# A hybrid decoder step on one core: prompt attention's sums of values in undivided float32, two tiles of keys in the two halves of TensorE's columns

## The chip, the cores and the metric

The program runs on 1 core of one Trainium2 chip. The time is device microseconds of one execution; lower is better. All times below are of this one core.

## The reference, cut to what matters

One decoder layer runs on 1024 prompt tokens and on 8 sampled tokens with 8192 tokens of cache each. The prompt's attention has three branches (compressed keys, selected blocks, a window of 512), 8 heads in 2 groups and a head size of 64. For 1024 tokens all 16 blocks are selected, so the selected branch is plain causal attention over all keys. Each branch takes a softmax, and the three sums of values are gated and added:

```python
s_c = jnp.einsum('bqgrd,bcgd->bgrqc', q, kc).astype(f32) + bias_c
p_c = jax.nn.softmax(jnp.where(valid_c, s_c, NEG), axis=-1) * valid_c
o_c = jnp.einsum('bgrqc,bcgd->bqgrd', p_c.astype(vc.dtype), vc)
...
o_s = jnp.einsum('bgrqk,bgqkd->bqgrd', p_s.astype(v_sel.dtype), v_sel)
...
o_w = jnp.einsum('bgrql,blgd->bqgrd', p_w.astype(vw.dtype), vw)
g = jax.nn.sigmoid(gates)
o = g[..., 0:1] * o_c + g[..., 1:2] * o_s + g[..., 2:3] * o_w
```

Everything is float32.

## The kernel before

The kernel goes through projections, retention, keys and values, then a stage in which the prompt's attention is woven together with the compression of the 8 caches and the sampled tokens' attention, and then output projection, feed-forward network and embedding. Large products are made in a split form: a float32 operand x is kept as hi = x rounded to float32r and lo = x - hi, and products of such parts are added up in PSUM. Other products (the compression, L944, the transposes, L1144) take undivided float32 operands.

**Prompt attention** works in 32 units: 8 tiles i of 128 queries, 2 groups, 2 pairs of heads. A unit has two heads, so the moving operand of its sums of values is 128 keys by 256 (two heads by 128 queries). `near_scores` and `far_scores` make scores, exponentials (ScalarE) and the scaling by gate and sum; `near_values` sums the compressed tile and up to 5 tiles of the window, `far_values` sums i + 1 tiles of keys. Both call `values`, which takes the tiles of keys two at a time (a part): PE transposes the probabilities of a part into a PSUM tile `t` (L1144); ScalarE casts them to `ph` (L1149), VectorE subtracts to get `pl` (`sub` at L142); `products` then multiplies. Over a unit the parts number half its tiles, rounded up, for near and far each: 80 near and 80 far parts in all, 136 of two tiles and 24 of one, 296 tiles.

In `products` the stationary operand is a tile of values from `vst` or `cvst`: 128 keys by 128 columns, the 64 hi columns and the 64 lo columns side by side. It is multiplied once with `ph` and once with `pl`; the PSUM bank `o` thus has the hi part of the values in its rows 0 to 63 and the lo part in its rows 64 to 127, and `far_values` adds the two halves (`ot`, `mo`).

**The stage's other work on PE.** The compression's products (L944, 128 by 128 stationary, 256 moving columns, float32), transposes and score products of the sampled tokens (L1258, L1268), and the compression's tails (L1200, and L1207 with L1208). L1200, L1207 with L1208, and L1268 already write two halves: each pair has two stationary operands of 64 columns, one for PSUM rows 0 to 63 and one for rows 64 to 127 of the same bank.

**What sets the order.** `weave` calls the generators of the stage by the costs that they yield; a list scheduler in the framework then sets each engine's final order. Each engine runs its own list strictly in that order and waits on semaphores. PSUM tiles `t` have 2 buffers, `o` has 1, `ph` and `pl` have 2 each.

Of the kernel before, what the change touches and what calls it, by code (L numbers as in the profile page):

```python
# [11 lines left out]
F32R = mybir.dt.float32r  # L12
# [28 lines left out]
def f32(ap):  # L41
    return ap.bitcast(F32)
# [78 lines left out]
def hybrid_kernel(tc, I, C, O):  # L121
    nc = tc.nc
    V, G, A, P, SY = nc.vector, nc.gpsimd, nc.scalar, nc.tensor, nc.sync
# [6 lines left out]
    def tl(pool, shape, tag, dt=F32, bufs=None):  # L130
        kw = {} if bufs is None else {"bufs": bufs}
        return pool.tile(shape, dt, tag=tag, name=nm(tag), **kw)
# [8 lines left out]
    def sub(eng, out, a, b):  # L141
        eng.tensor_tensor(out=out, in0=a, in1=b, op=ALU.subtract)  # L142
# [537 lines left out]
    for pair in range(2):  # L680
        rqk = tl(pr, [128, 2, 2, T], "rqk", bufs=1)
        rgs = tl(pr, [128, 2, T], "rgs", bufs=1)
        if pair:
# [3 lines left out]
            for t in range(9):  # L687
                pt, r = tok_major(wts, 256, t)
# [12 lines left out]
    pq = pool("pq", side="right")  # L701
# [1 line left out]
    pcv = pool("pcv", side="right")  # L703
    pat = pool("pat", side="right")
    ckst = [tl(pat, [128, 64], f"ckst{g}", F32R) for g in range(2)]
    cvst = tl(pat, [128, 2, 128], "cvst", F32R)
    cfar = const(pat, "cfar")
    rowv = const(pat, "rowv")
    vst = tl(pq, [128, 2, 8, 2, 128], "vst", F32R)

    kst = [tl(pq, [128, 2, S], f"kst{g}", F32R) for g in range(2)]
    pb = pool("pb")
# [41 lines left out]
    def keys_values(kind, ncol):  # L754
        wts = w_take()
        pend, kds = [], []

        def turn(t, pair):
            cs = slice((t - 1) * 128, (t + 1) * 128)
            ptr = bank("t", 2)  # L760
            for i in range(2):
                P.transpose(ptr[:, i * 128:(i + 1) * 128], pair[i], ident)
            for g in range(2):
                gh, gl = slice(g * 64, g * 64 + 64), slice(64 - g * 64, 128 - g * 64)
                A.copy(kst[g][gh, kind, cs], ptr[gh, :256])
                sub(V, kst[g][gl, kind, cs], ptr[gh, :256], f32(kst[g][gh, kind, cs]))

        for t in (8, *range(8)):
            pt, r = tok_major(wts, ncol, t)
            kv = tl(pb, [128, 256], "kv", bufs=4)  # L770
            A.copy(kv[:r], pt[:r, 0:256])
            if kind == 1:
                th = tl(pb, [128, 24], "gth", bufs=2)
                A.activation(th[:r], pt[:r, 256:280], AF.Tanh, scale=0.5)
            vr = kv[:, 128:256]
            if t < 8:
                hi, lo = vst[:, kind, t, :, 0:64], vst[:, kind, t, :, 64:128]
                vr3 = vr.rearrange("p (g d) -> p g d", g=2)
                A.copy(hi, vr3)
                sub(V, lo, vr3, f32(hi))  # L780
            else:
                A.copy(vnew[:, kind, :], vr[:r])
            sq = tl(pb, [128, 128], "sq", bufs=1)
            A.activation(sq[:r], kv[:r, 0:128], AF.Square)
            ssk = tl(pb, [128, 2], "ssk", bufs=2)
            V.reduce_sum(ssk[:r], sq[:r].rearrange("p (g d) -> p g d", g=2), axis=AX)
            rsqrt_small(ssk[:r], ssk[:r], 1.0 / 64, 2, r)
            t1 = tl(pb, [128, 2, 64], "kt1", bufs=2)
            mul(V, t1[:r], kv[:r, 0:128].rearrange("p (g d) -> p g d", g=2), ssk[:r].unsqueeze(2).to_broadcast([r, 2, 64]))
            ko = tl(pb, [128, 2, 64], "ko", bufs=4)  # L790
            mul(V, ko[:r], t1[:r], kn_bc[:r].unsqueeze(1).to_broadcast([r, 2, 64]))
            kflat = ko[:r].rearrange("p g d -> p (g d)")
            names = ("slc_k", "slc_v") if kind == 0 else ("win_k", "win_v")
            for n, src in zip(names, (kflat, vr[:r])):
                if t == 8:
                    dst = O["s_" + n][0, :, 0] if kind == 0 else O["s_" + n][0, :, 511]
                elif kind == 0:
                    dst = O["p_" + n][0, 0, t * 128:(t + 1) * 128]
                elif t >= 4:
                    dst = O["p_" + n][0, 0, t * 128 - 512:(t + 1) * 128 - 512]  # L800
                else:
                    continue
                SY.dma_start(dst.rearrange("t g d -> t (g d)"), src)
            if kind == 1:
                G.tensor_scalar(gsig[:r, t, :], th[:r], 0.5, 0.5, op0=ALU.mult, op1=ALU.add)
            if 3 <= t < 7:
                w_split()
            yield 2700.0
            if t == 8:
                knew = kflat  # L810
            if t == 0:
                ptr = bank("t", 2)
                P.transpose(ptr[:, :8], knew, ident[:8, :8])
                V.tensor_copy(knT[:, kind, :], ptr[:, :8])
            if pend and t % 2 == 0:
                turn(*pend)
                pend = []
            if t < 8:
                kds.append(kflat)
                if t % 2 == 1:  # L820
                    pend, kds = (t, kds), []
        yield 1500.0
        turn(*pend)
# [33 lines left out]
    def prompt_blocks():  # L857
        staged = stage_w1(pb, pcw, 0)
        for kv in (0, 1):
# [28 lines left out]
            if kv == 0:  # L888
                sq = tl(ptb, [64, 2, 64], "csq")
                A.activation(sq, pt3, AF.Square)  # L890
                ssk = tl(ptb, [64, 2], "css")
                V.reduce_sum(ssk, sq, axis=AX)
                rsqrt_small(ssk, ssk, 1.0 / 64, 2, 64)
                mul(V, sq, pt3, ssk.unsqueeze(2).to_broadcast([64, 2, 64]))
                mul(V, sq, sq, kn_bc[:64].unsqueeze(1).to_broadcast([64, 2, 64]))
                yield 2500.0
                pt = bank("r", 3)
                P.transpose(pt[:, :64], sq.rearrange("p g d -> p (g d)"), ident[:64, :64])
                for g in range(2):
                    gh, gl = slice(g * 64, g * 64 + 64), slice(64 - g * 64, 128 - g * 64)  # L900
                    A.copy(ckst[g][gh], pt[gh, :64])
                    sub(V, ckst[g][gl], pt[gh, :64], f32(ckst[g][gh]))
            else:
                G.memset(f32(cvst[64:128]), 0.0)
                A.copy(cvst[:64, :, 0:64], pt3)
                sub(V, cvst[:64, :, 64:128], pt3, f32(cvst[:64, :, 0:64]))
        fetch(0, 0)

    weave((chain(keys_values(0, 256), keys_values(1, 280)), 1.0), (prompt_blocks(), 1.0))
# [121 lines left out]
    class Unit:  # L1031
# [96 lines left out]
            sel = [(0, nt - 4), (nt - 4, 4)] if nt > 4 else [(0, nt)]  # L1128
            yield from u.branch(1, sel, 0, u.psel, 0)

        def products(u, ph, pl, part, last):
            for x, st in enumerate(part):
                P.matmul(u.po[:, :256], st[2], ph[:, x, :], start=u.done == 0, stop=False)  # L1133
                u.done += 1
                P.matmul(u.po[:, :256], st[2], pl[:, x, :], start=False, stop=last and x == len(part) - 1)

        def values(u, steps, last):
            pend = None
            for n in range(0, len(steps), 2):
                part = steps[n:n + 2]  # L1140
                pt = bank("t", NT)
                for x, (src, c0, _) in enumerate(part):
                    for r in range(2):
                        P.transpose(pt[:, (x * 2 + r) * 128:(x * 2 + r + 1) * 128], src[:, r, c0:c0 + 128], ident)  # L1144
                w = len(part) * 256
                ph = tl(pp, [128, 2, 256], "ph", F32R, bufs=2)
                pl = tl(pp, [128, 2, 256], "pl", F32R, bufs=2)
                ptv = pt[:, :w].rearrange("p (x n) -> p x n", n=256)
                A.copy(ph[:, :len(part)], ptv)  # L1149
                sub(V, pl[:, :len(part)], ptv, f32(ph[:, :len(part)]))  # L1150
                yield w * 0.85
                if pend:
                    u.products(*pend, False)
                    yield 430.0
                pend = (ph, pl, part)
            yield 600.0
            u.products(*pend, last)

        def near_values(u):
            u.po, u.done = bank("o", 1), 0  # L1160
            steps = [(u.pcm, 0, cvst[:, u.g, :])]
            steps += [(u.pwin, (j - u.w0) * 128, vst[:, 1, j, u.g, :]) for j in range(u.w0, u.nt)]
            yield from u.values(steps, False)

        def far_values(u):
            yield from u.values([(u.psel, j * 128, vst[:, 0, j, u.g, :]) for j in range(u.nt)], True)
            ot = tl(pp, [64, 256], "ot", bufs=1)
            A.copy(ot, u.po[64:128, :256])
            mo = tl(pp, [128, 128], "mo", bufs=2)
            for par in range(2):  # L1170
                add(V, mo[par * 64:(par + 1) * 64], u.po[0:64, par * 128:(par + 1) * 128], ot[:, par * 128:(par + 1) * 128])
            SY.dma_start(mix_d[u.g * 2 + u.r0 // 2][:, u.i * 128:(u.i + 1) * 128], mo)
# [920 lines left out]
```

## Time and profile before

| what | value |
|---|---|
| runs of the kernel | 2142.01, 2144.17, 2145.64 us; median 2144.17 |
| profiled execution | 2140.78 us, its span 2139.0 us |
| granted TensorE clock, mean over the span | 0.986 |
| attention's sums (tile `o`) | from 460.7 to 1174.7 us of the span |

The span is the time from the first to the last instruction. A matmul's record in the trace begins when its data begin to flow and ends at a modelled end, and records of following matmuls overlap; how much of PE one instruction takes is therefore read from the distance of starts or of ends, not from a record's length. PEld is the loading of the stationary operand, which runs beside PE. A float32 matmul appears as two records on PE under the same line, one for each of its two passes, and a float32r matmul as one.

### The profile page before, as it was taken

What the parts mean: (1) busy time and instruction counts of PE and PEld (TensorE: products, weight loads), DVE (VectorE), ACT (ScalarE), POOL (GpSimd) and SP (SyncE); (2) the same over time, 40 slices, a digit from 0 to 9 for tenths busy, and PEclk for the clock granted to TensorE, in tenths of its full rate; (3) what the DMA queues carried; (4) which work ended last, traced back from release to release, by engine and by line L of the source; (5) the groups of instructions that cost most, each with busy time, mean ns of one, the idle gap of its engine ahead of it and who ended that gap; (6) DMA issues with size and microseconds to landing.
All of it is one profiled execution on the core that took longest, in us unless ns stands there. A gap on an engine that the chain in (4) does not pass through costs nothing.

```text
span 2139.0 us, 38497 instructions
## 1 busy us (share of the span) xinstructions
PE 2045.0 (96%) x14824; PEld 1895.3 (89%) x14824; DVE 1370.5 (64%) x3135; ACT 843.5 (39%) x2091; POOL 690.6 (32%) x891
## 2 busy tenths in 40 slices
PE   7999999979999999999999898999999999999998
PEld 6998998867788886679999798999999999999998
DVE  4335145357778889677665458766666676878632
ACT  3331222236565654554444334323323335542321
POOL 1235334277777765757673033000000000000100
PEclk9999999989999999999999998999999999999999
DMA  6322223244334343644541731233233244553221
GB/s 225 136 73 74 75 69 87 59 125 134 106 117 123 109 126 109 204 145 143 158 153 44 218 95 47 94 122 107 79 112 102 85 141 147 179 154 125 91 74 50
DMA packets 186032, 246.77 MB, mean 115 GB/s; under 512 B 17252, under 2 KB 155144, under 8 KB 185656
## 3 DMA queue, kind: packets, MB, share of 16 engines
q1 hardware_dynamic: 160760, 160.40, 24.4%
q0 software_dynamic: 25088, 83.90, 12.6%
q8 instruction: 117, 1.92, 0.4%
q14 instruction: 67, 0.55, 0.1%
HBM read 204.09 MB, written 44.34 MB: 116 GB/s over the span
## 4 chain that ended last, share of the span: by engine, by line
PE 53%; DVE 6%; DMA 4%; ACT 1%; issue 1%; POOL 0%; DVEq 0%; ACTq 0%; POOLq 0%; SPq 0%
PE m L944 8%; PE s L157 5%; PE s L159 5%; PE s L158 5%; PE m L157 4%; PE m L159 4%; PE m L158 4%; PE t L157 3%; PE t L159 3%; PE t L158 3%; PE t L1144 2%; DMA wst<-act_d 2%; DVE x L142 1%; PE o L1133 1%; PE s L1268 1%
## 5 line engine op out<-in xcount | busy, mean ns | idle before, releaser
L944 PE MATMUL m<-seg,w1h 128*128 128x256 f32 x1024 | 296.3, 396 | 0.8 <-DVE scl L1048 0.8
L157 PE MATMUL s<-x,wu 128*128 128x258 f32 x872 | 248.9, 286 | 5.3 <-ACT x L152 3.3
L158 PE MATMUL s<-x,wu 128*128 128x258 f32 x872 | 248.5, 285 | 1.0 <-DVE x L142 0.9
L159 PE MATMUL s<-x,wu 128*128 128x258 f32 x872 | 247.8, 284 | 0.5 <-DVE wu L142 0.5
L142 POOL TENSOR_TENSOR x<-h,x 128x516 fp32r<-128x516 f32 x4 | 5.7, 1415 | 676.9 <-ACT x L152 676.9
L157 PE MATMUL m<-x,wu 128*128 128x258 f32 x768 | 218.9, 286 | 2.6 <-DVE h L148 1.5
L158 PE MATMUL m<-x,wu 128*128 128x258 f32 x768 | 218.1, 284 | 2.5 <-DVE x L142 2.5
L159 PE MATMUL m<-x,wu 128*128 128x258 f32 x768 | 217.9, 284 | 0.0
L944 PEld LDWEIGHTS m<-seg,w1h 128*128 128x128 f32 x1024 | 173.9, 194 | 20.8 <-issue 8.9
L152 ACT CAST wu<-wu 128x512 fp32r<-128x512 f32 (+2 forms) x178 | 109.6, 626 | 193.4 <-DVE wu L142 119.1
L953 DVE STREAM_TRANSPOSE seg<-raw 128x1024 f32<-128x1024 f32 x128 | 158.6, 1240 | 37.5 <-PE m L944 29.9
L157 PEld LDWEIGHTS s<-x,wu 128*128 128x128 f32 x872 | 165.8, 190 | 6.3 <-ACT x L152 3.7
L158 PEld LDWEIGHTS s<-x,wu 128*128 128x128 f32 x872 | 166.5, 191 | 1.6 <-DVE x L142 1.4
L159 PEld LDWEIGHTS s<-x,wu 128*128 128x128 f32 x872 | 166.4, 191 | 0.7 <-DVE wu L142 0.7
L142 DVE TENSOR_TENSOR wu<-wu,wu 128x512 fp32r<-128x512 f32 (+2 forms) x178 | 126.6, 715 | 61.7 <-ACT wu L152 60.1
L157 PE MATMUL t<-x,wu 128*128 128x258 f32 x528 | 150.8, 286 | 7.3 <-DVE h L148 4.9
L290 PE MATMUL g<-wh,xnh 128*128 128x256 f32 (+3 forms) x504 | 148.9, 296 | 2.5 <-ACT xnh L340 2.3
L158 PE MATMUL t<-x,wu 128*128 128x258 f32 x528 | 149.6, 283 | 0.5 <-DVE x L142 0.4
L159 PE MATMUL t<-x,wu 128*128 128x258 f32 x528 | 149.4, 283 | 0.3 <-DVE wu L142 0.3
L157 PEld LDWEIGHTS m<-x,wu 128*128 128x128 f32 x768 | 146.1, 190 | 4.0 <-issue 1.7
L158 PEld LDWEIGHTS m<-x,wu 128*128 128x128 f32 x768 | 146.6, 191 | 2.7 <-DVE x L142 2.7
L854 POOL DMA_INDIRECT raw<-in_cache_cmp_v_dram,cix x128 | 126.6, 989 | 66.9 <-issue 28.5
(474 smaller groups left out, 5977.8 us busy)
## 6 DMA issues: line engine op xcount, KB each, us to landing
act_d<-act SPq DMA_DIRECT2D x22, 903.0 KB
wr<-in_w_in_dram SPq DMA_DIRECT2D x12, 1024.0 KB
wu<-in_w_gate_dram SPq DMA_DIRECT2D x22, 512.0 KB
wu<-in_w_up_dram SPq DMA_DIRECT2D x22, 512.0 KB
st<-act_d SPq DMA_DIRECT2D x42, 258.0 KB
wu<-in_w_down_dram SPq DMA_DIRECT2D x16, 512.0 KB
wst<-act_d SPq DMA_DIRECT2D x28, 258.0 KB
mr<-mix_d SPq DMA_DIRECT2D x16, 258.0 KB
```

Source lines behind the costliest of these rows:

```text
L142: eng.tensor_tensor(out=out, in0=a, in1=b, op=ALU.subtract)
L152: A.copy(hi, src)
L157: P.matmul(out, wh, xh, start=first, stop=False, **kw)
L158: P.matmul(out, wh, xl, start=False, stop=False, **kw)
L159: P.matmul(out, wl, xh, start=False, stop=last, **kw)
L290: P.matmul(pt[:r, :n], xh, wh[:, k, :n], start=k == 0, stop=False)
L854: G.indirect_dma_start(out=raws[n, par][:, x, :], out_offset=None, in_=crow[kv], in_offset=bass.IndirectOffsetOnAxis(ap=cix[:, par, col:co ...
L944: P.matmul(out, w[:, k, :], x[:, k // 2 % 2, :, k % 2, :], start=first and k == 0, stop=k == 7, skip_group_check=not first)
L953: V.transpose(t.rearrange("p k (x d) -> p k x d", x=4), raws[n, par][:, :, s2 * 256:(s2 + 1) * 256].rearrange("p x (k d) -> p k x d", k=8))
L1133: P.matmul(u.po[:, :256], st[2], ph[:, x, :], start=u.done == 0, stop=False)
L1144: P.transpose(pt[:, (x * 2 + r) * 128:(x * 2 + r + 1) * 128], src[:, r, c0:c0 + 128], ident)
L1268: P.matmul(pt[x * 64:(x + 1) * 64, :256], qzb[:, b, :], kt[:, x * 256:(x + 1) * 256], start=True, stop=True)
```

## The change

Values are kept as they are: `vst` and `cvst` become plain float32 with 64 columns, and the transposed probabilities are copied once, to `pv`, in float32; `ph`, `pl` and the subtraction are gone. A part's first tile of keys goes to PSUM rows 0 to 63 and its second one to rows 64 to 127, each with one float32 matmul of 64 stationary columns. The two halves are added at the unit's end as before, by the same instructions. The yields that set the weaving are the same.

```diff
-    cvst = tl(pat, [128, 2, 128], "cvst", F32R)
+    cvst = tl(pat, [128, 2, 64], "cvst")
...
-    vst = tl(pq, [128, 2, 8, 2, 128], "vst", F32R)
+    vst = tl(pq, [128, 2, 8, 2, 64], "vst")
...
-                hi, lo = vst[:, kind, t, :, 0:64], vst[:, kind, t, :, 64:128]
-                vr3 = vr.rearrange("p (g d) -> p g d", g=2)
-                A.copy(hi, vr3)
-                sub(V, lo, vr3, f32(hi))
+                A.copy(vst[:, kind, t], vr.rearrange("p (g d) -> p g d", g=2))
...
-        def products(u, ph, pl, part, last):
+        def products(u, pv, part, last):
             for x, st in enumerate(part):
-                P.matmul(u.po[:, :256], st[2], ph[:, x, :], start=u.done == 0, stop=False)
+                P.matmul(u.po[x * 64:(x + 1) * 64, :256], st[2], pv[:, x, :], start=u.done < 2, stop=last[x])
                 u.done += 1
-                P.matmul(u.po[:, :256], st[2], pl[:, x, :], start=False, stop=last and x == len(part) - 1)
...
-                ph = tl(pp, [128, 2, 256], "ph", F32R, bufs=2)
-                pl = tl(pp, [128, 2, 256], "pl", F32R, bufs=2)
-                ptv = pt[:, :w].rearrange("p (x n) -> p x n", n=256)
-                A.copy(ph[:, :len(part)], ptv)
-                sub(V, pl[:, :len(part)], ptv, f32(ph[:, :len(part)]))
+                pv = tl(pp, [128, 2, 256], "pv", bufs=2)
+                A.copy(pv[:, :len(part)], pt[:, :w].rearrange("p (x n) -> p x n", n=256))
```

The order on PE at the end of one unit's far values (the twelfth unit; `o` is its bank of sums, `m` the compression, `t` under L1200 and L1207 the compression's tails; the line numbers of the changed kernel are 4 or 5 lower, so that L940 is L944 of before, L1195 is L1200, L1202 is L1207 and L1130 is the new matmul in `products`). Before:

```order
L944 MATMUL m_7485<-seg_7487,w1h_4131 128x256
L1200 MATMUL t_7632<-xh_7480,w_690_4142 64x256 x2
L1133 MATMUL o_7457<-ph_7605,vst_4068 128x256
L1135 MATMUL o_7457<-pl_7606,vst_4068 128x256
L1133 MATMUL o_7457<-ph_7605,vst_4068 128x256
L1135 MATMUL o_7457<-pl_7606,vst_4068 128x256
L1207 MATMUL t_7643<-ck_7635,qzk_5172 64x256
L1208 MATMUL t_7643<-csq_7637,c_bgsel_5170 64x256
L1133 MATMUL o_7457<-ph_7625,vst_4068 128x256
L1135 MATMUL o_7457<-pl_7626,vst_4068 128x256
L1067 MATMUL s_7658<-kst_674_4070,qa_7453 128x256
```

The same place in the changed kernel:

```order
L940 MATMUL m_7275<-seg_7277,w1h_4131 128x256 x2
L1130 MATMUL o_7251<-pv_7369,vst_4068 64x256 x2
L940 MATMUL m_7275<-seg_7277,w1h_4131 128x256
L1141 MATMUL t_7394<-c_ident_66,psel_7191 128x128 x2
L940 MATMUL m_7275<-seg_7277,w1h_4131 128x256
L1195 MATMUL t_7402<-xh_7270,w_690_4142 64x256 x2
L1130 MATMUL o_7251<-pv_7381,vst_4068 64x256 x2
L1130 MATMUL o_7251<-pv_7397,vst_4068 64x256
L1202 MATMUL t_7411<-ck_7405,qzk_5155 64x256
L1203 MATMUL t_7411<-csq_7407,c_bgsel_5153 64x256
L1063 MATMUL s_7425<-kst_674_4070,qa_7247 128x256
```

Four matmuls of 128 columns for a part of two tiles became two of 64 columns that stand side by side (x2), and the part of one tile became one. Here the tails of the compression stand directly beside them. Over the whole program the 296 new matmuls stand in 160 unbroken groups of 64-column matmuls: in 25 of the groups a tail or a score product of the sampled tokens stands too, as both do here, and in the other 135 the new ones stand alone between matmuls of 128 columns.

The order on VectorE at the same unit, where `pl` is the low part of the probabilities, `seg` the transposes and differences for the compression, and `xh` and `sacc` belong to its tails. Before:

```order
L953 STREAM_TRANSPOSE seg_7715<-raw_7518 128x1024
L142 TENSOR_TENSOR pl_7579<-t_7573,ph_7578 128x512
L142 TENSOR_TENSOR pl_7590<-t_7584,ph_7589 128x512
L142 TENSOR_TENSOR seg_7719<-seg_7614,seg_7715 128x1024
L827 SCALAR_TENSOR_TENSOR xh_7480<-ch_t_7609,m_7229 128x2x128
L142 TENSOR_TENSOR pl_7606<-t_7600,ph_7605 128x512
L142 TENSOR_TENSOR pl_7626<-t_7622,ph_7625 128x256
L953 STREAM_TRANSPOSE seg_7722<-raw_7518 128x1024
```

In the changed kernel:

```order
L949 STREAM_TRANSPOSE seg_7476<-raw_7302 128x1024
L142 TENSOR_TENSOR seg_7480<-seg_7388,seg_7476 128x1024
L824 SCALAR_TENSOR_TENSOR xh_7270<-ch_t_7383,m_7035 128x2x128
L949 STREAM_TRANSPOSE seg_7483<-raw_7302 128x1024
L148 TENSOR_TENSOR mo_7418<-o_7251,ot_7416 64x128
```

The four subtractions are gone and nothing takes their place.

## Rows read from the trace of the kernel before

**Rows 1.** The page's first part: busy us, share of the span, instructions.

```profile
PE 2045.0 (96%) x14824; PEld 1895.3 (89%) x14824; DVE 1370.5 (64%) x3135; ACT 843.5 (39%) x2091; POOL 690.6 (32%) x891
```

**Rows 2.** Stretches: from:to, length, busy us of each engine (instructions), granted clock, DMA.

```profile
365.00:441.00 76.00, 68.00 (x521) 63.21 (x520) 30.92 (x100) 25.01 (x102) 21.24 (x49) 0.96 0.34 76
455.00:565.00 110.00, 99.83 (x525) 79.59 (x524) 80.92 (x199) 58.57 (x176) 86.30 (x101) 0.94 0.40 123
565.00:797.00 232.00, 228.63 (x1330) 189.55 (x1329) 187.66 (x457) 137.77 (x412) 175.59 (x206) 1.00 0.39 118
797.00:962.00 165.00, 155.93 (x931) 114.73 (x929) 130.62 (x347) 84.61 (x219) 98.92 (x116) 0.99 0.48 151
962.00:1180.00 218.00, 216.52 (x1418) 198.31 (x1418) 139.44 (x328) 92.57 (x262) 131.46 (x148) 1.00 0.41 127
```

**Rows 3.** Tile o alone, 455 to 1180 us: PE, PEld, DVE, ACT.

```profile
455.00:1180.00 725.00, 134.52 (x592) 91.17 (x592) 17.87 (x64) 11.79 (x32) 0.99 0.42 129
```

**Rows 4.** PE's timeline around 566 us: start us, us, instructions; a part of two tiles.

```profile
565.85 0.60 PE L944 MATMUL m<-seg,w1h 128*128 128x256 f32 x2
566.09 0.47 PE L1133 MATMUL o<-ph,vst 128*128 128x256 f32 x1
566.40 0.28 PE L1135 MATMUL o<-pl,vst 128*128 128x256 f32 x1
566.52 0.28 PE L1133 MATMUL o<-ph,vst 128*128 128x256 f32 x1
566.63 0.28 PE L1135 MATMUL o<-pl,vst 128*128 128x256 f32 x1
566.75 1.03 PE L944 MATMUL m<-seg,w1l 128*128 128x256 f32 x4
```

**Rows 5.** PE's timeline around 577 us: two float32 matmuls of 64 columns.

```profile
576.55 0.28 PE L1068 MATMUL s<-kst,qb 128*128 128x256 f32 x1
576.75 0.43 PE L1207 MATMUL t<-ck,qzk 128*64 128x256 f32 x1
576.76 0.43 PE L1208 MATMUL t<-csq,c_bgsel 128*64 128x256 f32 x1
577.02 0.38 PE L1207 MATMUL t<-ck,qzk 128*64 128x256 f32 x1
577.03 0.38 PE L1208 MATMUL t<-csq,c_bgsel 128*64 128x256 f32 x1
577.34 0.70 PE L944 MATMUL m<-seg,w1h 128*128 128x256 f32 x2
```

**Rows 6.** PE's timeline around 758 us: one such matmul alone.

```profile
758.11 0.34 PE L1068 MATMUL s<-kst,qb 128*128 128x384 f32 x1
758.38 0.65 PE L1208 MATMUL t<-csq,c_bgsel 128*64 128x256 f32 x2
758.95 0.70 PE L944 MATMUL m<-seg,w1h 128*128 128x256 f32 x2
```

**Rows 7.** Groups of instructions by shape, 455 to 1180 us, and vst's of the whole span.

```profile
L142 DVE TENSOR_TENSOR pl<-t,ph 128x512 fp32r<-128x512 f32 x136 | 92.3, 682 | 29.0 <-ACT ph L1149 28.5
L1149 ACT CAST ph<-t 128x512 fp32r<-128x512 f32 x136 | 79.3, 586 | 80.1 <-PE t L1144 71.6 <-DVE pn L1475 2.2 <-DVE seg L953 2.1
L1261 ACT COPY w1l<-t 128x512 f32<-128x512 f32 x40 | 23.4, 587 | 27.7 <-PE t L1258 27.0 <-PE s L1268 0.5
L142 DVE TENSOR_TENSOR pl<-t,ph 128x256 fp32r<-128x256 f32 x24 | 10.0, 416 | 7.6 <-ACT ph L1149 7.6
...
L142 DVE TENSOR_TENSOR vst<-kv,vst 128x128 fp32r<-128x128 f32 x16 | 4.5, 289 | 15.1 <-ACT vst L779 15.0
```

**Rows 8.** What PE waited for, 455 to 1180 us: total us, times, longest.

```profile
PE t L1144 <- POOL pwin L1057: 8.1, 7, 2.9
PE s L1268 <- ACT psel L1095: 2.2, 1, 2.2
PE t L1144 <- POOL pcm L1057: 1.8, 1, 1.8
PE t L1144 <- DVE pl L142: 1.8, 2, 1.4
```

More of the change, by code (lines that the diff above doesn't have):

```diff
@@ L903, in prompt_blocks @@
             else:
-                G.memset(f32(cvst[64:128]), 0.0)
-                A.copy(cvst[:64, :, 0:64], pt3)
-                sub(V, cvst[:64, :, 64:128], pt3, f32(cvst[:64, :, 0:64]))
+                G.memset(cvst[64:128], 0.0)
+                A.copy(cvst[:64], pt3)
         fetch(0, 0)
@@ L1145, in values @@
                 w = len(part) * 256
-                ph = tl(pp, [128, 2, 256], "ph", F32R, bufs=2)
-                pl = tl(pp, [128, 2, 256], "pl", F32R, bufs=2)
-                ptv = pt[:, :w].rearrange("p (x n) -> p x n", n=256)
-                A.copy(ph[:, :len(part)], ptv)
-                sub(V, pl[:, :len(part)], ptv, f32(ph[:, :len(part)]))
+                pv = tl(pp, [128, 2, 256], "pv", bufs=2)
+                A.copy(pv[:, :len(part)], pt[:, :w].rearrange("p (x n) -> p x n", n=256))
                 yield w * 0.85
                 if pend:
-                    u.products(*pend, False)
+                    left = len(steps) - n
+                    u.products(*pend, (False, last[1] and left < 2))
                     yield 430.0
-                pend = (ph, pl, part)
+                pend = (pv, part)
             yield 600.0
@@ L1162, in near_values @@
             steps += [(u.pwin, (j - u.w0) * 128, vst[:, 1, j, u.g, :]) for j in range(u.w0, u.nt)]
-            yield from u.values(steps, False)
+            yield from u.values(steps, (False, u.nt < 2))
         def far_values(u):
-            yield from u.values([(u.psel, j * 128, vst[:, 0, j, u.g, :]) for j in range(u.nt)], True)
+            yield from u.values([(u.psel, j * 128, vst[:, 0, j, u.g, :]) for j in range(u.nt)], (True, u.nt > 1))
             ot = tl(pp, [64, 256], "ot", bufs=1)
```

## The prediction

> **What bounds the kernel now.** I read the page's busy shares first, then the stage of the change in stretches, then its groups of instructions, and last PE's timeline, to price single instructions. PE is busy for 96% of the span and VectorE for 64% [rows 1], but a mean over stages doesn't say what ends a wait in this one. The sums of values run from 455 to 1180 us. The four stretches there hold 725 us with 700.9 us of PE busy (99.83, 228.63, 155.93, 216.52), so PE idles for 24.1 us: 10.2 in the first stretch, 3.4, 9.1 and 1.5 in the others [rows 2]. VectorE is busy for 538.7 us, 74% of the stage [rows 2]. So the stage is PE's. What the change adds on PE lengthens the run nearly one for one, and what it takes from VectorE is worth at most what PE waits. Most of PE's longest waits are not for the operation that goes: 8.1 us for GpSimd's scaling of the window's probabilities, 2.2 us and 1.8 us for other inputs, and 1.8 us for `pl` [rows 8].
>
> **Removed on PE.** The sums take 592 matmuls on PE [rows 3], two for each of 296 tiles. Within a part they start 0.12, 0.11 and 0.12 us after one another (566.40, 566.52, 566.63, then the compression at 566.75), on average 0.117 us, though each record is 0.28 us long [rows 4]. The same comes out by ends: the two L944 ahead end at 565.85 + 0.60 = 566.45, the four behind at 566.75 + 1.03 = 567.78. Two more L944 make a record 1.03 - 0.60 = 0.43 us longer, so four take 0.86, and the part took 1.33 - 0.86 = 0.47 us, or 4 x 0.117 [rows 4]. Removed: 592 x 0.117 = 69 us.
>
> **Added on PE.** The count of passes doesn't fall: 296 float32 matmuls of two passes are 592 records again. A saving can only come from two tiles in two halves of the columns. The trace of before has this very form: L1207 and L1208, two stationary operands of 64 columns, two moving operands of 256 columns, the two halves of one bank. Their first passes start 0.01 us apart, and so do their second ones [rows 5]: the halves do run together. But the pair isn't joined to its neighbours. L1068 ahead ends at 576.55 + 0.28 = 576.83, the two L944 behind end at 577.34 + 0.70 = 578.04. Of these 1.21 us the two L944 need 0.43, so the pair costs 0.78 us [rows 4, 5]. The streams of its two passes are 0.43 of it; the other 0.35 are gaps where PE goes over to half columns (576.75, when L1068 would have let the next matmul start 0.12 after 576.55) and back again (the record of L944 is 0.70 where it is 0.60 in an unbroken run, and begins 0.31 after the pair's second pass) [rows 4, 5]. One half alone isn't cheaper: L1208 by itself stands between ends at 758.45 and 759.65, 1.20 us, less 0.43: 0.77 us [rows 6].
>
> The subtractions count the parts: 136 of two tiles and 24 of one [rows 7]. A part of two tiles goes from 0.47 to 0.78 us, 136 x 0.31 = 42 us; a part of one tile from 2 x 0.117 = 0.235 to 0.77 us, 24 x 0.535 = 13 us. Together +55 us. The order of the changed kernel puts 25 of the groups directly beside tails or score products of the same 64 columns, where the way there and back need only be paid once. No row shows two such pairs in succession, so a joint group saves between 0 and 0.35 us: 0 to 9 us in all. I take 7, since nothing has to be switched between them. PE: **+48 us**, bounds 46 and 55.
>
> **A rule of the Trainium skill beside this.** The row prices a pair among other matmuls at 0.78 us. The page "TensorE: Matmul & The Clock Gate", section "Part 3: Packing small matmuls", gives packed matmuls the length of one matmul and some 4 ns for each further tile; by it the 160 parts would cost what their streams cost, and the sum would lose its +48. The page "TensorEngine Tiling (Array Packing)", section "Tiling Modes", says on the other side that a change of the tiling mode drains TensorE, without a price. The trace has both: 0.01 us between the halves, and the 0.35 us around them.
>
> **Given back by VectorE.** 160 subtractions go, 92.3 + 10.0 = 102.3 us [rows 7], 19% of VectorE's stage. Named waits of PE for `pl` are 1.8 us [rows 8]. Beyond that VectorE's queue gets shorter ahead of the minima, the sums and the transposes for the compression, and GpSimd's scaling, the longest wait, starts on VectorE's sums earlier. A slower PE also leaves the others more slack. The bounds: nothing, and all 24 us of idle time with the 6.6 us that the lower clock costs in the first stretch (a granted 0.94 over 110 us [rows 2] is 13 us at 1.2 in place of 2.4 GHz, half of it lost), 31 us. The other stretches stand at 0.99 and 1.00. I take **-10 us**, since the named waits are nearer to the lower end.
>
> **At nothing.** ScalarE's copy to `pv`: 586 ns for the cast now, 587 ns for a plain copy of the same shape (L1261) [rows 7]. PSUM tile `t` is free after the copy, not after the subtraction; that is in the -10. The 16 subtractions into `vst`, 4.5 us [rows 7], lie between 365 and 441 us, where VectorE is busy for 30.9 of 76 us and PE for 68.0 [rows 2]: the cover is PE's projections, and 4.5 us is all that it could be. Loads of weights become shorter but PEld, 582 us of the stage's 725 [rows 2], is not what PE waits for in the run of [rows 4].
>
> **Sum.** 2140.8 us for the profiled execution (span 2139.0 and 1.8 around it) + 48 - 10 = 2179. The median of the runs is 3.4 us above that execution, so I forecast **2181 us** for a median, +1.7%. A measurement of this kernel can tell about 0.2%, 4 us, from no change.
>
> **Rivals.**
> - *The gaps aren't paid (faster).* If the groups ran into their neighbours, a part would cost its streams, 0.43 us: 160 x 0.43 = 69 us, what was removed, and VectorE's relief of 10 to 31 us would be the gain: 2113 to 2134. It decides below 0.49 us for a part (69 us and the 10 of relief over 160). This is what the clock-gate page's packing rule gives. Against it stand both priced rows: 0.78 and 0.77 [rows 5, 6]. 5%.
> - *The halves don't run together when they accumulate.* L1207 and L1208 write once, the new matmuls add up over a unit. A pair would then cost two streams of 0.43 and the gaps, 1.21 us, 136 x 0.43 = 58 us more: about 2239. Nothing in the rows makes an accumulating matmul slower: L1133 and L1135 accumulate at 0.117 us. 4%.
> - *Waits given back in full.* The relief is 20 to 31 us and not 10: 2159 to 2171. For it speaks that VectorE stands behind the scaling's inputs; against it, that most waits are named for GpSimd and ScalarE. 17%.
> - *A new wait.* A part's matmuls now stand as one block in PE's order, so all of them wait for `pv`; before, the hi product of a tile and the compression's could fill in. If a fifth of the 160 blocks waits for 0.6 us, a copy's length, that is 19 us: 2190 to 2206. PE orders are in line, so the compression behind waits too. 15%.
>
> My forecast has the remaining 59%, with 2168 to 2192 for itself (give-back 0 to 20, joint groups 0 to 9 us).
>
> **Range.** From the full give-back to the new wait: 2158 to 2204. Faster by over 0.2% is the first rival, 5%; within 0.2% would take a give-back of over 40 us, more than PE idles: 3%; slower 92%.
>
> **What would show it.** In the profile after: 592 records for tile `o` on PE with 64 columns, starts 0.01 us apart within a part; ends around such a part that are 1.21 us apart where two L944 follow; no `pl`; VectorE's busy time in the stage down by some 100 us while the stage gets longer by 35 to 45; PE's idle time down from 24 to about 15 us; stages before 455 us and behind the attention unchanged. I am wrong if the gap around a part is well under 0.35 us, if halves start one after the other, or if the stage's idle time on PE falls or grows by more than 15 us.

## The result and the profile after

| kernel | median us (lowest to highest, runs) | ratio to before, 95% interval |
|---|---|---|
| before | 2144.9 (2142.01 to 2148.67, 4) | 1 |
| changed | 2169.47 (2168.17 to 2171.24, 4) | 1.0123 [1.0105, 1.0141] |

The change makes the kernel slower by 24.6 us between medians (by the ratio, with which the experiments are compared below, 26 us), where the forecast had 38 us from the profiled execution (2179) and 36 us between medians (2181). The profiled execution of the changed kernel took 2170.63 us, its span is 2168.9 us. Between the two profiled executions lie 29.9 us, more than between the medians, since that of before lies 4 us below its own median; some 3 of them lie behind the attention, where no instruction changed.

The page's first part after the change, to be read beside [rows 1]:

```profile
PE 2076.9 (96%) x14824; PEld 1849.3 (85%) x14824; DVE 1279.4 (59%) x2958; ACT 843.4 (39%) x2091; POOL 686.9 (32%) x891
```

PE has the same count of records, VectorE 91 us less to do and 177 instructions fewer (160 into `pl`, 17 into `vst` and `cvst`), and PE 32 us more.

The stretches of the stage, beside [rows 2] (from:to, length, busy us of PE, PEld, DVE, ACT, POOL, granted clock, DMA). The first two are cut at the same times as there, and the changed kernel is some 3 us behind in its work at 565 and some 11 us at 797; the other two cuts, 975 and 1206, stand where the same work is done as at 962 and 1180 before:

```profile
455.00:565.00 110.00, 99.46 (x513) 68.67 (x514) 67.59 (x173) 57.26 (x176) 86.18 (x100) 0.95 0.41 123
565.00:797.00 232.00, 231.26 (x1272) 163.61 (x1270) 148.08 (x373) 132.74 (x394) 167.05 (x198) 1.00 0.37 111
797.00:975.00 178.00, 171.70 (x1007) 117.39 (x1008) 124.61 (x346) 91.32 (x240) 107.30 (x127) 0.99 0.48 149
975.00:1206.00 231.00, 229.79 (x1415) 186.61 (x1413) 112.30 (x279) 92.95 (x262) 128.22 (x147) 1.00 0.39 121
```

The stage is 751 us long where it was 725. PE is busy for 732.2 of them, 31.3 us more than before, and idle for 18.8, 5.3 us less; VectorE is busy for 452.6, 86 us less. So the stage grows by 26 us; it is PE's before and after.

A part in the changed kernel, on PE's timeline (start us, us, instruction), beside [rows 4] and [rows 5]:

```profile
565.64 0.60 PE L940 MATMUL m<-seg,w1h 128*128 128x256 f32 x2
566.17 0.65 PE L1130 MATMUL o<-pv,vst 128*64 128x256 f32 x4
566.75 1.13 PE L940 MATMUL m<-seg,w1h 128*128 128x256 f32 x4
```

Read by ends as in the prediction: the two L940 ahead end at 566.24, the four behind at 567.88; of these 1.64 us four L940 need 0.86, so the part costs 0.78 us, what L1207 and L1208 cost before [rows 5]. Of the 0.78 us, 0.43 are streams. The other 0.35 can be read off the lines: the part starts 0.10 us after the two L940 ahead have streamed (565.64 + 0.43 = 566.07), the four L940 behind start 0.15 us after the part has streamed (566.17 + 0.43 = 566.60), and their record is 1.13 us long where it is 1.03 in an unbroken run.

A part beside a score product of the sampled tokens, which has half columns too:

```profile
896.62 0.61 PE L1253 MATMUL t<-c_ident,slc 128*128 128x128 f32 x4
897.16 0.65 PE L1130 MATMUL o<-pv,vst 128*64 128x256 f32 x4
897.64 0.60 PE L1263 MATMUL s<-w1l,qzb 128*64 128x256 f32 x4
```

The transposes end at 897.23, the part at 897.81 and the score product at 898.24. The second pair adds 0.43 us, its streams alone: between two groups of the same column width there is no gap. That price had no row before.

What PE waited for in the stage (total us, times, longest), beside [rows 8]:

```profile
PE t L1141 <- POOL pwin L1053: 7.0, 5, 3.6
PE m L940 <- DVE xh L824: 4.0, 2, 3.4
PE t L1141 <- POOL pcm L1053: 1.8, 1, 1.8
```

The waits for `pl` are gone, the longest one, for GpSimd's scaling, stands.

### The profile page after: what moved, and what is told of

Read it like the earlier page. It is cut to its first block, busy times and chain, and to the rows that moved or that the text cites. A ratio compares the mean times of both kernels' runs of the same rounds, so it can differ in the third digit from the quotient of the medians.

```text
span 2168.9 us, 38334 instructions
## 1 busy us (share of the span) xinstructions
PE 2076.9 (96%) x14824; PEld 1849.3 (85%) x14824; DVE 1279.4 (59%) x2958; ACT 843.4 (39%) x2091; POOL 686.9 (32%) x891
## 4 chain that ended last, share of the span: by engine, by line
PE 61%; DVE 5%; DMA 4%; issue 1%; ACT 1%; POOL 1%; ACTq 0%; DVEq 0%; SPq 0%; POOLq 0%
PE m L940 13%; PE s L157 5%; PE s L158 5%; PE s L159 5%; PE m L157 4%; PE m L159 4%; PE m L158 4%; PE o L1130 3%; PE t L1141 3%; PE t L157 2%; PE t L159 2%; PE t L158 2%; PE s L1063 1%; DMA wst<-act_d 1%; DVE x L142 1%
## 5 line engine op out<-in xcount | busy, mean ns | idle before, releaser
L940 PE MATMUL m<-seg,w1h 128*128 128x256 f32 x1024 | 296.9, 397 | 1.5 <-DVE scl L1044 1.5
L940 PEld LDWEIGHTS m<-seg,w1h 128*128 128x128 f32 x1024 | 172.0, 192 | 40.1 <-issue 29.8
L940 PE MATMUL m<-seg,w1l 128*128 128x256 f32 x512 | 147.5, 398 | 4.0 <-DVE xh L824 4.0
```

What stands on the lines that cost most here:

```text
L940: P.matmul(out, w[:, k, :], x[:, k // 2 % 2, :, k % 2, :], start=first and k == 0, stop=k == 7, skip_group_check=not first)
```

## The experiments

All ratios are to the kernel before, run on the same chip beside each experiment; a per cent of the time is 21.45 us. A difference between two rows, or between a row and the changed kernel's 1.0123, is sure to 0.2 to 0.3%, 4 to 6 us. Three tests take the forecast's sum apart: the relief of VectorE (e1, e2, e5), the price of half columns (e3, e4, e6, e7), and the two terms as a whole (e8, e9). The last two (e10, e11) look for use of the freed VectorE.

| run | what | median us | ratio, 95% interval |
|---|---|---|---|
| e1 | before, no subtraction | 2140.57 | 0.9964 [0.9951, 0.9977] |
| e2 | before, subtraction made but not read | 2143.15 | 0.9982 [0.9970, 0.9994] |
| e3 | changed, one half of the columns only | 2227.79 | 1.0383 [1.0358, 1.0407] |
| e4 | changed, all 128 columns | 2195.58 | 1.0226 [1.0204, 1.0248] |
| e5 | changed, subtraction kept | 2176.63 | 1.0163 [1.0146, 1.0180] |
| e6 | changed, products grouped by call | 2154.5 | 1.0051 [1.0034, 1.0068] |
| e7 | changed, products grouped by unit | 2142.39 | 1.0001 [0.9991, 1.0010] |
| e8 | before, sums left out | 2101.06 | 0.9745 [0.9727, 0.9763] |
| e9 | changed, sums left out | 2103.07 | 0.9757 [0.9737, 0.9776] |
| e10 | e7, window's scaling on VectorE | 2154.95 | 0.9998 [0.9985, 1.0010] |
| e11 | before, window's scaling on VectorE | 2157.26 | 1.0011 [0.9994, 1.0027] |

(The kernel before had medians of 2147.78 us beside e1 to e4, 2142.89 beside e5 to e7 and 2153.99 beside e8 to e11; so ratios are compared, not medians.)

**e1, the relief alone.**

```diff
-                pl = tl(pp, [128, 2, 256], "pl", F32R, bufs=2)
...
-                sub(V, pl[:, :len(part)], ptv, f32(ph[:, :len(part)]))
...
-                pend = (ph, pl, part)
+                pend = (ph, ph, part)
```

> The kernel before, without the subtraction that makes pl; both matmuls of a tile read ph, so the low part of the probabilities is left out of the sums. PE has the same instructions, VectorE 160 (102 us) fewer: the relief by itself. My theory now (the parts cost what the forecast said, and the relief gives back more than the 10 us taken): 18 to 25 us faster than before, 2120 to 2127. First rival (the forecast's give-back is right, and a part costs less than 0.78 us in the changed kernel): 10 us faster, 2135. Second rival (the relief gives nothing, the changed order of instructions does): within 4 us of before.

It is faster by 0.36%, 7.7 us. My theory fell at its first test: the relief is not 18 to 25 us. It is near the 10 us that the forecast had taken (the interval is 5 to 10.5 us). In the stage of that run VectorE is busy for 451.55 us, where it was 538.7 [rows 2]:

```profile
455.00:1178.00 723.00, 693.78 (x4198) 579.71 (x4199) 451.55 (x1170) 373.57 (x1071) 486.71 (x569) 0.99 0.42 129
```

PE idles for 29 us there, 5 us more than before, though the stage is shorter: taking 87 us from VectorE doesn't end PE's waits, which are mostly for GpSimd and ScalarE [rows 8].

**e2, the subtraction unread.**

```diff
-                pend = (ph, pl, part)
+                pend = (ph, ph, part)
```

> As the run without the subtraction, both matmuls of a tile read ph, but VectorE still makes pl, which nothing reads. It splits the relief: VectorE's work and the hold on the PSUM tile t are as before, but PE no longer waits for pl. If the relief comes from PE's own waits for pl: as fast as the run without the subtraction, 2120 to 2127. If it comes from VectorE's queue, and from t coming free earlier: within 4 us of before, 2141 to 2149. A mixture lies between, and its place says how much each gives.

Faster by 0.18%, 3.9 us: about half of the relief would be PE's wait for `pl`, the rest VectorE's queue and the earlier free `t`. The intervals of the two runs overlap, so the split isn't shown.

**e5, the subtraction kept in the changed kernel.**

```diff
+                ptv = pt[:, :w].rearrange("p (x n) -> p x n", n=256)
+                pl = tl(pp, [128, 2, 256], "pl", bufs=2)
-                A.copy(pv[:, :len(part)], pt[:, :w].rearrange("p (x n) -> p x n", n=256))
+                A.copy(pv[:, :len(part)], ptv)
+                sub(V, pl[:, :len(part)], ptv, pv[:, :len(part)])
```

> The changed kernel with VectorE's subtraction kept, into a tile that nothing reads: 160 subtractions of 0.68 and 0.42 us, 102 us of VectorE, and t held until they end. The counterpart of taking it away from the kernel before. If the relief of VectorE's queue made up for a part of the loss: 10 to 23 us slower than the changed kernel, 2179 to 2192. If the relief was only PE's wait for pl, or the new order: within 4 us of 2169.

1.0163 against 1.0123: 0.40%, 8.6 us slower than the changed kernel (3 to 14), a little below the 10 to 23 that were expected. From either side the relief is about 8 us.

**e3, one half.**

```diff
-                P.matmul(u.po[x * 64:(x + 1) * 64, :256], st[2], pv[:, x, :], start=u.done < 2, stop=last[x])
+                P.matmul(u.po[0:64, :256], st[2], pv[:, x, :], start=u.done == 0, stop=last[0] and x == len(part) - 1)
...
-            A.copy(ot, u.po[64:128, :256])
+            A.copy(ot, u.po[0:64, :256])
```

> The changed kernel with all tiles summed in PSUM rows 0 to 63, none in the other half (the final addition then adds the one half to itself, so the sums come out doubled; the instructions are the same in number). Theory (two halves run together): a part of two tiles costs two streams, 0.43 us more, 136 of them: 58 us slower than the changed kernel, about 2228; some waits may be covered, so 2215 to 2230. Rival (halves don't overlap when they accumulate, and the price of a part came from elsewhere): within 5 us of the changed kernel's 2169.

1.0383 against 1.0123: 2.60%, 55.8 us for 136 x 0.43 = 58 us of streams. The two halves do run together when they accumulate, and a microsecond of stream is worth 0.95 of one in time (with the error of the difference, 0.85 to 1.07). A part in that run takes 1.08 us of record where the changed kernel has 0.65:

```profile
702.08 1.03 PE L940 MATMUL m<-seg,w1h 128*128 128x256 f32 x4
703.04 1.08 PE L1130 MATMUL o<-pv,vst 128*64 128x256 f32 x4
```

**e4, all 128 columns.**

```diff
-    vst = tl(pq, [128, 2, 8, 2, 64], "vst")
+    vst = tl(pq, [128, 2, 8, 2, 128], "vst")
+    G.memset(vst[:, :, :, :, 64:128], 0.0)
...
-                P.matmul(u.po[x * 64:(x + 1) * 64, :256], st[2], pv[:, x, :], start=u.done < 2, stop=last[x])
+                P.matmul(u.po[:, :256], st[2], pv[:, x, :], start=u.done == 0, stop=last[0] and x == len(part) - 1)
```

> The changed kernel with stationary operands of all 128 columns: 64 of values and 64 of zeros, one undivided float32 matmul for each tile into all rows of the bank. No change to half columns and back, but no two tiles together either. Theory (streams 0.43 us for a tile, gaps of 0.35 us only where the column width changes): 296 x 0.432 = 128 us against about 116 in the changed kernel, 12 us slower than it: 2178 to 2185. Rival (the gap comes with undivided float32 or with the wait for pv, not with half columns): 160 gaps of 0.35 us stay, 2230 to 2240. Rival (half columns cost nothing beyond the streams): also 2228.

(`cvst` is widened and cleared in the same way.) 1.0226, 22 us above the changed kernel, where 12 were expected and 60 by the rivals. The gap is gone from the timeline:

```profile
705.73 1.89 PE L941 MATMUL m<-seg,w1l 128*128 128x256 f32 x8
707.46 1.03 PE L1131 MATMUL o<-pv,vst 128*128 128x256 f32 x4
708.13 0.53 PE L1064 MATMUL s<-kst,qa 128*128 128x384 f32 x1
```

L941 ends at 707.62 and the part at 708.49: 0.87 us, two tiles of 0.43, nothing around them. So the gap belongs to the change of the column width and not to undivided float32. The run has 296 x 0.43 = 127 us of streams for the 69 of the changed kernel, 58 us more; at 0.95 (e3) these are 55, and it lost 22. So the gaps that it saves gave 33 us. They are not 160: the tails and score products of the other work keep theirs. Counted in the traces, the stage has 205 unbroken runs of half-column records on PE in the changed kernel and 72 in this one, so 133 runs went, for 0.25 us each, not 0.35.

**e6 and e7, fewer groups.** The first (e6) holds a call's copies and issues their products together, in `release`, a new function; the second (e7) also holds the near ones until the unit's far ones. The diff is that of e6, cut to the place of the call; `pv` has 6 buffers in e6 and 9 in e7.

```diff
-                if pend:
-                    left = len(steps) - n
-                    u.products(*pend, (False, last[1] and left < 2))
-                    yield 430.0
-                pend = (pv, part)
-            yield 600.0
-            u.products(*pend, last)
+                held.append((pv, part))
+            yield 600.0 + 430.0 * (total - 1)
+            u.release(held, last)
...
```

> The changed kernel with the products of all parts of one call (near or far) issued together after the last transposes of the call, and 6 buffers of pv: 66 groups of half-column matmuls on PE in place of 160, the same matmuls. Theory (0.35 us for each change of the column width and back): the sums cost 69 us of streams and 66 x 0.35 = 23, against 116 us: 24 us faster than the changed kernel, 2145, as fast as before; 2140 to 2152 with new waits. Rival (the cost goes with the matmuls or the parts, not with the groups): 2165 to 2173.

> As the run with products grouped by call, but the near products are held until the unit's far ones, with 9 buffers of pv: 35 groups. Theory: 69 + 35 x 0.35 = 81 us against 116 in the changed kernel, 35 us faster than it, 2134, and 10 us faster than before; 2128 to 2145 with new waits, since the unit's end now has all its products behind one another. Rival (the cost doesn't go with the groups): 2165 to 2173.

Grouped by call the kernel is 0.72% faster than the changed one, 15.4 us where 24 were expected, and 0.5% slower than before; grouped by unit it is 1.22% faster, 26.2 us where 35 were expected, and as fast as before. So the cost goes with the groups, as the theory says, but not at 0.35 us. The groups alone (94 and 125 fewer) are not the right count here either, since fewer tails and score products now stand beside a group: in all, the stage has 76 runs of half-column records on PE before, 205 in the changed kernel, 128 in e6 and 102 in e7. For each run saved it is 0.20 us in e6 (77 fewer) and 0.25 us in e7 (103 fewer), to 0.04 to 0.07 us either way. One group of e7, a unit of 13 tiles:

```profile
704.46 1.03 PE L940 MATMUL m<-seg,w1h 128*128 128x256 f32 x4
705.42 0.43 PE L1130 MATMUL o<-pv,cvst 128*64 128x256 f32 x1
705.43 0.43 PE L1130 MATMUL o<-pv,vst 128*64 128x256 f32 x1
705.69 0.38 PE L1130 MATMUL o<-pv,cvst 128*64 128x256 f32 x1
705.69 2.96 PE L1130 MATMUL o<-pv,vst 128*64 128x256 f32 x23
708.59 0.38 PE L1063 MATMUL s<-kst,qa 128*128 128x256 f32 x1
```

From the end of L940 at 705.49 to that of L1063 at 708.97 it is 3.48 us; L1063 needs 0.12 of them, and the other 3.36 are seven parts of 0.43 (3.02) and one gap of 0.34. On PE's timeline the gap's price holds to the hundredth; in the kernel's time it doesn't.

**e8 and e9, the sums left out.**

```diff
-                P.matmul(u.po[:, :256], st[2], ph[:, x, :], start=u.done == 0, stop=False)
-                u.done += 1
-                P.matmul(u.po[:, :256], st[2], pl[:, x, :], start=False, stop=last and x == len(part) - 1)
+                if u.done == 0:
+                    P.matmul(u.po[:, :256], st[2], ph[:, x, :], start=True, stop=False)
+                    P.matmul(u.po[:, :256], st[2], pl[:, x, :], start=False, stop=True)
+                u.done += 1
...
-                P.matmul(u.po[x * 64:(x + 1) * 64, :256], st[2], pv[:, x, :], start=u.done < 2, stop=last[x])
+                if u.done < 2:
+                    P.matmul(u.po[x * 64:(x + 1) * 64, :256], st[2], pv[:, x, :], start=True, stop=True)
```

> The kernel before with the sums of values left out but for the first tile of each unit: 528 of the 592 matmuls go; copies, subtractions and transposes stay. It measures the term that the forecast called removed. By the burst's 0.117 us each: 62 us faster than before, 2083. By the average that the trace of before has from end to end over all of these matmuls, 0.136 us (84.6 us less 4.3 us that belong to half-column groups ahead, over 592): 72 us faster, 2073. If PE gets short enough to wait for VectorE, which keeps its subtractions, less than either.

> The changed kernel with the sums left out but for the first tile in each half of each unit, 64 of 296 matmuls: it measures the term that the forecast called added. The forecast's 117 us for all, less 32 groups of 0.78 that stay (25 us): 92 us faster than the changed kernel, 2078. Against the kernel before without its sums, it should be faster by VectorE's relief, some 8 us, if that is what the runs without and with the subtraction showed, or slower by some us, if the two kernels differ in another way.

Without 528 of the old matmuls the time is 2.55% lower, 55 us; their price is 62 at 0.117 us each, and 72 at the 0.136 that they took from end to end. Without 232 of the 296 new ones it is lower than the changed kernel's by 3.66% of the time before, 79 us; their price is 92. Both terms are worth less in time than on PE, by 7 and 13 us, to 4 and 6 us either way. Their difference, 24 us, is nearly the change's whole loss (26 us by the ratio). The two kernels without the sums are within their error of one another (0.9745 and 0.9757). The expectation had the changed one faster there by VectorE's relief, but it left out that the two runs don't keep the same: e9 keeps 32 pairs, 25 us on PE, and e8 only 64 old matmuls, 7 us. To be level with 18 us more on PE, e9 must gain elsewhere, and the relief of 8 us would be part of it. The stages of the two runs (first e8, then e9):

```profile
455.00:1137.00 682.00, 644.84 (x3653) 518.68 (x3654) 525.39 (x1328) 371.16 (x1070) 489.32 (x569) 0.97 0.44 136
```

```profile
455.00:1139.00 684.00, 652.71 (x3735) 516.19 (x3736) 453.12 (x1170) 373.23 (x1071) 488.83 (x570) 0.98 0.45 138
```

PE idles for 37 us in the one and 31 in the other, where before it was 24: with less on PE the other engines' chains show, and a part of what was taken from PE is waited for after all. The clock is a second reason: TensorE goes at 1.2 or 2.4 GHz, and the mean grant over the executions was 0.982 of the upper level in both runs, against 0.985 in those of the kernel before beside them. Where PE had work in that time, this is up to 6 us by e8 and 5 by e9.

**e10 and e11, use of the freed VectorE.** The first is e7 with the window's scaling moved from GpSimd to VectorE, the second the kernel before with the same move.

```diff
-W_ATT, W_ATT2, W_DEC, W_VAL, W_RET, W_SP, W_T, ON, ORD = 1.6, 1.8, 0.5, 1.0, 3.0, (9000.0, 0.0, 6000.0, 0.0), (4000.0, 9000.0), "GAG", (0,7,1,6,2,5,3,4)
+W_ATT, W_ATT2, W_DEC, W_VAL, W_RET, W_SP, W_T, ON, ORD = 1.6, 1.8, 0.5, 1.0, 3.0, (9000.0, 0.0, 6000.0, 0.0), (4000.0, 9000.0), "GAV", (0,7,1,6,2,5,3,4)
...
-                    G.tensor_scalar(dst[:, r, :width], dst[:, r, :width], scl[:, r:r + 1], gate[r], op0=ALU.mult, op1=ALU.mult)
+                    (V if ON[br] == "V" else G).tensor_scalar(dst[:, r, :width], dst[:, r, :width], scl[:, r:r + 1], gate[r], op0=ALU.mult, op1=ALU.mult)
```

> The products grouped by unit, and the window's scaling by gate and sum on VectorE in place of GpSimd (64 operations of 128 by up to 640). PE's longest named wait is for that scaling, 5.4 us in the run grouped by unit and 8.1 in the kernel before; VectorE has 102 us less to do. If the wait is what it seems: 4 to 8 us faster than grouped by unit alone, 2135 to 2139, and faster than before. Rival (VectorE's queue then delays the minima and the transposes by as much): within 4 us of it, 2139 to 2146.

> The control for the run before it: the kernel before, with the window's scaling on VectorE, which still makes its 160 subtractions. If room on VectorE is what makes the move pay: no gain or a loss here, 2143 to 2155. If the move pays by itself: 4 to 8 us faster, 2137 to 2141.

Neither differs from the kernel before. The longest named wait is gone, and others have its place: in e10 PE waits longest for `pv` (5.3 us, twice) and for the compression's copy (4.9 us, once). A wait's total is not what its removal gives.

No version was found that beats the kernel before; e7 equals it.

## Why the prediction was right in kind and too high in size

- **PE is the bound.** Right: the stage grew by 26 us with PE's busy time up by 31 and its idle time down by 5.
- **Removed, 69 us.** The price, 0.117 us a matmul, is that of an unbroken part. Left out, they gave 0.89 of it (e8: 55 of 62), a part of the rest may be the clock. But in the kernel before they took more than that price: from end to end 84.6 us, or 80 without the 4 that belong to half-column groups ahead of them. The 11 us above 69 stand mostly at matmuls that follow other work.
- **Added, 117 us.** The group's price of 0.78 us is right to the hundredth, halves together and gaps around (the timeline after, e3, e4): counted as in the prediction, the 111 pairs that stand alone in the trace after average 0.78 us, and all groups together come to about 116 us. A joint group saves the whole 0.35 us, at the upper end of its bounds: 25 x 0.35 = 9 us in place of 7.
- **The step that failed** is the first paragraph's "nearly one for one", by which the +48 us on PE stood in the sum at full worth. The streams barely change (69 us of old ones, 160 x 0.43 = 69 of new ones), so the +48 were gaps alone. And gaps didn't count in full: a microsecond of stream costs 0.95 in time (e3), a gap of 0.35 us costs 0.20 to 0.25 (e4, e6, e7). For the change itself it is 24.6 us and 8 of relief over 129 more runs of half columns, again 0.25 us. Of 129 x 0.35 = 45 us of gaps the time shows 33. That a gap counts for less than its length is clear of the noise; that it counts for less than a stream is likely, not shown.
- **Given back, 10 us.** Right in size: 7.7 us by taking the subtraction away before (e1), 8.6 us by putting it back after (e5).
- **The signs named.** 592 records of 64 columns, halves 0.01 us apart, no `pl`, VectorE down by 86 us: as named, near enough. The stage's growth of 26 us lies under the 35 to 45 named, and PE's idle time, 18.8 us, over the 15. The stages around the attention are unchanged but for some 3 us behind it.
- **The rivals.** Gaps unpaid (5%) is refuted by the timeline; halves one after the other (4%) by e3; a new wait of the blocks for `pv` (15%) isn't among PE's longest waits. The time lies inside the forecast's own 2168 to 2192, at its lower end, and also where "waits given back in full" had put it (2159 to 2171), but that rival's mechanism, VectorE's relief of 20 to 31 us, didn't come: it stayed at 8 us.
- **A sum that doesn't fit.** The 2192 at the upper end of its own range is too low for the bounds named beside it: with nothing given back and no saving in joint groups it is 2181 + 10 + 7 = 2198. Nothing hangs on it here.

The Trainium skill's page "TensorEngine Tiling (Array Packing)" (section "Tiling Modes") says that a change of tiling mode drains TensorE. The trace agrees in that such a change costs time: 0.34 to 0.35 us for the way there and back, once a group whatever its length. That the gap is a drain, no run here shows. The packing rule of the Trainium skill's page "TensorE: Matmul & The Clock Gate" (section "Part 3: Packing small matmuls") holds inside a group alone: there a pair adds 0.43 us, one stream.

**What stays open** is what covers a third of each gap. It is not the relief (e1, e5). The traces show where the time went, though no run tries it by itself. The old matmuls took 80 us from end to end, 11 above their price; the wide ones of e4, counted the same way, take 138 us where their streams are 128; the half-column groups take about 116 us, nothing above their price. The 138 - 116 = 22 us are what e4 lost against the changed kernel. So on PE's timeline the change is 116 - 80 = +36 us and not +48, and with 10 us less at PE's other work this is the stage's 26. A part that starts after other work seems to wait for a weight or a copy at full width too, and the gap runs while it would have waited. Against a simple exchange stands e8: leaving the old matmuls out gave 55 us and not 72, so such waits don't all go with the matmuls. A second estimate, over the whole stage, points the same way: take each PE record's distance of ends from the one ahead of it, and call the lower quartile for its shape and the shape ahead its price (a group as one). The prices rise by some 40 us, and what lies above them falls from about 50 us by some 15, about 6 of these at the sums' own records and 6 to 8 at the transposes.

## What to carry to other kernels

Count how often the instructions in order change the width of the stationary operand, not only how long they stream: two half-column matmuls run together for the price of one, but each group that stands alone among full-width matmuls pays for the way there and back, so such products are to be issued in long groups. Here even one group a unit (e7) only won back the loss. Price a term on the bounding engine by a row, and then its worth in time by leaving it out: here streams counted at 0.95 and gaps at 0.6 to 0.7. Look up, too, what the instructions that go take from end to end where they stand (here 80 us), not only in an unbroken run (69). Relief of an engine that is busy for three quarters of a stage gave 8 us for 102 us of work.

## What was not expected of the hardware

Half-column groups of different tiles and different banks follow one another without a gap: 0.43 us for the second pair, and 3.36 us, one gap included, for seven parts in one group. A microsecond of gap on TensorE was worth 0.6 to 0.7 in the kernel's time, each value to 0.1 to 0.2, where one of streaming was worth 0.95, to 0.1.
